# RMSNorm with GELU on one core: the first group's store in two pieces, gamma in four transfers, the last group in four stores

## The chip, the cores and the metric

One NeuronCore of one Trainium2 chip. The metric is the device time of the slowest core in microseconds (us), here of the only core. A lower number is better. The profile is of one execution; its "span" is from the first to the last instruction.

## The reference

x is 8 x 1024 x 2048 in float32, gamma has 2048 elements.

```python
rms = np.sqrt(np.mean(x ** 2, axis=-1, keepdims=True) + eps)
out = gamma * x / rms
return 0.5 * out * (1 + np.tanh(np.sqrt(2 / np.pi) * (out + 0.044715 * out ** 3)))
```

67.1 MB are read and 67.1 MB written; nothing of that can be saved.

## The kernel before

The 8192 rows are cut into 16 groups of 128 partitions x 4 rows. A partition's four rows are 32 KB in one piece, in memory and in the slot. There are six slots. SP issues the loads on one DMA queue, ACT gamma and the stores on another.

```python
store_pieces = {G - 1: [(0, 2), (2, 2)]}          # last group: two stores of 2 MiB

def load(g):
    nc.sync.dma_start(out=slot[g % SLOTS], in_=x3[g])
# ... squares (ACT), inverse_rms (POOL), scale by gamma (DVE)
def gelu_store(g):
    for r, n in store_pieces.get(g, [(0, R)]):
        for q in range(r, r + n):
            # ... Gelu of row q on ACT, in place
        nc.scalar.dma_start(
            out=o3[g, :, r : r + n, :], in_=slot[g % SLOTS][:, r : r + n, :]
        )

with tc.manual_schedule():
    for g in range(SLOTS):
        load(g)
    nc.scalar.dma_start(                            # gamma: one transfer of 8 KB
        out=gamma_row[:, :, 0:GW],
        in_=gamma.rearrange("(o a b) -> o a b", o=1, b=GW),
    )
    # ... memsets, gamma spread over the partitions by matmuls
    for g in range(G + 1):
        if g < G:
            squares(g); inverse_rms(g); scale(g)    # (one statement per line in the kernel)
        if g:
            gelu_store(g - 1)
            if g - 1 + SLOTS < G:
                load(g - 1 + SLOTS)
```

Of the kernel before, what the change touches and what calls it, by code (L numbers as in the profile page):

```python
# [1 line left out]

# [4 lines left out]

FP32 = mybir.dt.float32
ALU = mybir.AluOpType
ACT = mybir.ActivationFunctionType  # L10

P = 128
ROWS = 4
SLOTS = 6

GW = 128


@with_exitstack
def kernel(  # L20
    ctx: ExitStack,
    tc: tile.TileContext,
    x: bass.AP,
    gamma: bass.AP,
    eps: bass.AP,
    out: bass.AP,
):




    nc = tc.nc
    D = x.shape[-1]
    R = ROWS
    eps_f = float(eps)
    x3 = x.rearrange("b s d -> (b s) d").rearrange("(g p r) d -> g p r d", p=P, r=R)
    o3 = out.rearrange("b s d -> (b s) d").rearrange("(g p r) d -> g p r d", p=P, r=R)
    G = x3.shape[0]

    sbuf = ctx.enter_context(tc.tile_pool(name="sbuf", bufs=1))  # L40
    psum = ctx.enter_context(
        tc.tile_pool(name="psum", bufs=1, space=bass.MemoryType.PSUM)
    )
    slot = [sbuf.tile([P, R, D], FP32, name=f"slot{i}") for i in range(SLOTS)]
    gamma_row = sbuf.tile([1, D // GW, GW + 16], FP32, name="gamma_row")
    ones = sbuf.tile([1, P], FP32, name="ones")
    warm = sbuf.tile([1, 1], FP32, name="warm")
    power = sbuf.tile([P, R], FP32, name="power")
    ssq = sbuf.tile([P, G, R], FP32, name="ssq")
    rstd = sbuf.tile([P, G, R], FP32, name="rstd")  # L50
    ms = sbuf.tile([P, R], FP32, name="ms")
    y = sbuf.tile([P, R], FP32, name="y")
    z = sbuf.tile([P, R], FP32, name="z")
    gamma_ps = psum.tile([P, D], FP32, name="gamma_ps")
    junk = psum.tile([P, D], FP32, name="junk")

    store_pieces = {G - 1: [(0, 2), (2, 2)]}
    scale_pieces = {G - 1: [(0, 1), (1, 1), (2, 1), (3, 1)]}

    def load(g):  # L60
        nc.sync.dma_start(out=slot[g % SLOTS], in_=x3[g])  # L61

    def squares(g):
        for r in range(R):
            nc.scalar.activation(  # L65
                out=junk,
                in_=slot[g % SLOTS][:, r, :],
                func=ACT.Square,
                accum_out=ssq[:, g, r : r + 1],
            )  # L70

    def scale(g):
        for r, n in scale_pieces.get(g, [(0, R)]):
            rows = slot[g % SLOTS][:, r : r + n, :]
            nc.vector.tensor_tensor(  # L75
                out=rows,
                in0=rows,
                in1=gamma_ps.unsqueeze(1).to_broadcast([P, n, D]),
                op=ALU.mult,
            )  # L80

    def inverse_rms(g):

        v = nc.gpsimd
        v.tensor_scalar(  # L85
            out=ms, in0=ssq[:, g, :], scalar1=1.0 / D, scalar2=eps_f,
            op0=ALU.mult, op1=ALU.add,
        )
        v.tensor_tensor(out=y, in0=ms, in1=power, op=ALU.pow)  # L89
        v.tensor_tensor(out=z, in0=y, in1=y, op=ALU.mult)  # L90
        v.tensor_tensor(out=z, in0=z, in1=ms, op=ALU.mult)  # L91
        v.tensor_scalar(  # L92
            out=z, in0=z, scalar1=-0.5, scalar2=1.5, op0=ALU.mult, op1=ALU.add
        )
        v.tensor_tensor(out=rstd[:, g, :], in0=z, in1=y, op=ALU.mult)  # L95

    def gelu_store(g):
        for r, n in store_pieces.get(g, [(0, R)]):
            for q in range(r, r + n):
                row = slot[g % SLOTS][:, q, :]  # L100
                nc.scalar.activation(  # L101
                    out=row, in_=row, func=ACT.Gelu_apprx_tanh,
                    scale=rstd[:, g, q : q + 1],
                )
            nc.scalar.dma_start(  # L105
                out=o3[g, :, r : r + n, :], in_=slot[g % SLOTS][:, r : r + n, :]
            )

    with tc.manual_schedule():
        for g in range(SLOTS):  # L110
            load(g)
        nc.scalar.dma_start(
            out=gamma_row[:, :, 0:GW],
            in_=gamma.rearrange("(o a b) -> o a b", o=1, b=GW),
        )
        nc.gpsimd.memset(power, -0.5)  # L116
        nc.vector.memset(warm, 0.0)  # L117
        nc.vector.memset(ones, 1.0)  # L118
        nc.scalar.activation(out=warm, in_=warm, func=ACT.Gelu_apprx_tanh)  # L119
        for k in range(0, D, 512):  # L120
            nc.tensor.matmul(  # L121
                out=gamma_ps[:, k : k + 512],
                lhsT=ones,
                rhs=gamma_row[:, k // GW : (k + 512) // GW, 0:GW],
                start=True,
                stop=True,
            )
        for g in range(G + 1):
            if g < G:
                squares(g)  # L130
                inverse_rms(g)
                scale(g)
# [6 lines that stand above are left out]
# [1 line left out]
_INS = ['x', 'gamma', 'eps']  # L140
_OUTS = [((8, 1024, 2048), 'float32')]

_NUMBERS = {'eps': 9.999999747378752e-06}


# [26 lines left out]
```

## Time and profile before

| what | value |
|---|---|
| median, lowest, highest of the first three timed runs | 317.68, 317.36, 317.83 us |
| the profiled run | 318.66 us, span 316.9 us |
| ACT busy | 251.1 us (79%) |
| DMA, mean over the span | 424 GB/s |

The page's DMA row has one digit per fortieth of the span: 9 means that the 16 DMA engines were busy 90% or more. A line of the windows view has the stretch, its length, the busy time of PE, weight load, DVE, ACT and POOL with instruction counts, the granted clock, and last the DMA share and GB/s. A packet's whole time and all its bytes are counted in the window in which it starts, so a window much shorter than a packet's 1.2 us swings, and a share above 1 there does not mean that an engine does more than one packet at a time. The lines themselves are shown in the prediction.

### The profile page before, as it was taken

To read this page: it belongs to the slowest core of one execution; us is meant where nothing else is said; L and a number is where in the kernel's file an instruction comes from. 1 tells how busy PE (TensorE), PEld (TensorE's weight loads), DVE (VectorE), ACT (ScalarE), POOL (GpSimd) and SP (SyncE) were. 2 spreads that over 40 slices of the span, in tenths; PEclk is the share of its full clock that TensorE was granted. 3 is DMA by queue.
4 is the path that set the end of the run, shared out by engine and by line. 5 is a ranking of instruction groups with operands and counts; after the bars stand their busy time and mean duration, and the time that the engine had idled before them with its cause. 6 is when DMAs were issued, how large, how long until landed. Compare 5 with 4: busy or idle time off the path is not lost.

```text
span 316.9 us, 473 instructions
## 1 busy us (share of the span) xinstructions
PE 7.2 (2%) x8; PEld 2.5 (1%) x8; DVE 139.4 (44%) x21; ACT 251.1 (79%) x194; POOL 32.3 (10%) x101
## 2 busy tenths in 40 slices
PE   0900000000000000000000000000000000000000
PEld 0300000000000000000000000000000000000000
DVE  0038909090919191732808246091550905582000
ACT  1379999999999997959689595995959859599800
POOL 0020102020202020202002020020200102001000
DMA  8999999999999999999999999999999999999995
GB/s 328 414 451 426 434 393 459 401 459 402 459 405 455 426 434 431 430 434 426 438 426 455 410 455 418 443 426 430 434 430 435 422 459 405 459 414 447 422 420 230
DMA packets 4787, 134.25 MB, mean 424 GB/s; under 512 B 544, under 2 KB 560, under 8 KB 560
## 3 DMA queue, kind: packets, MB, share of 16 engines
q1 hardware_dynamic: 2304, 67.11, 49.5%
q10 hardware_dynamic: 2480, 67.12, 49.1%
q14 instruction: 3, 0.02, 0.0%
HBM read 67.12 MB, written 67.11 MB: 424 GB/s over the span
## 4 chain that ended last, share of the span: by engine, by line
DMA 56%; ACT 33%; issue 5%; ACTq 1%; SPq 0%
DMA slot<-in_x_dram 30%; DMA out_dram<-slot 26%; ACT slot L101 19%; ACT junk L65 14%; ACTq L105 1%; SPq L61 0%; ACTq L101 0%; ACTq L65 0%
## 5 line engine op out<-in xcount | busy, mean ns | idle before, releaser
L75 DVE TENSOR_TENSOR slot<-slot,gamma_ps 128x8192 f32<-128x8192 f32 (+1 forms) x19 | 139.2, 7340 | 147.0 <-ACT junk L65 147.0
L65 ACT ACTIVATE junk<-slot 128x2048 f32<-128x2048 f32 x64 | 120.4, 1881 | 47.3 <-DMA slot<-in_x_dram 43.7
L101 ACT ACTIVATE slot<-slot,rstd 128x2048 f32<-128x2048 f32 x64 | 122.8, 1989 | 0.9 <-ACT slot L101 0.9
L85 POOL TENSOR_SCALAR ms<-ssq 128x4 f32<-128x4 f32 x16 | 3.1, 194 | 247.5 <-ACT junk L65 247.5
L89 POOL TENSOR_TENSOR y<-ms,power 128x4 f32<-128x4 f32 x16 | 16.1, 1009 | 1.3
L65 ACT ACTIVATION_READ_ACCUMULATOR junk<-slot 128x1 f32 x64 | 12.0, 188 | 0.0
L121 PE MATMUL gamma_ps<-gamma_row,ones 1*128 1x512 f32 x8 | 7.2, 1072 | 8.4 <-DMA gamma_row<-in_gamma_dram 8.4
L95 POOL TENSOR_TENSOR rstd<-z,y 128x4 f32<-128x4 f32 x16 | 3.2, 201 | 1.3
L91 POOL TENSOR_TENSOR z<-z,ms 128x4 f32<-128x4 f32 x16 | 3.2, 201 | 1.3
L90 POOL TENSOR_TENSOR z<-y 128x4 f32<-128x4 f32 x16 | 3.2, 199 | 1.3
L92 POOL TENSOR_SCALAR z<-z 128x4 f32<-128x4 f32 x16 | 3.1, 194 | 1.4
L121 PEld LDWEIGHTS gamma_ps<-gamma_row,ones 1*128 1x128 f32 x8 | 2.5, 325 | 11.5 <-issue 11.5
L119 ACT ACT_TABLE_LOAD x1 | 1.3, 1283 | 1.3 <-PEq L153 1.3
L117 DVE MEMSET warm<- 1x1 f32 x1 | 0.1, 59 | 0.8 <-PEq L153 0.8
L119 ACT ACTIVATE warm<-warm 1x1 f32<-1x1 f32 x1 | 0.2, 202 | 0.0
L118 DVE MEMSET ones<- 1x128 f32 x1 | 0.2, 165 | 0.0
L116 POOL MEMSET power<- 128x4 f32 x1 | 0.1, 102 | 0.3 <-POOLq L153 0.3
L153 POOL MEMSET const-float32-0.0<- 128x1 f32 x1 | 0.1, 99 | 0.2 <-issue 0.2
L153 POOL MEMSET const-bfloat16-1.0<- 128x1 bf16 x1 | 0.1, 102 | 0.0
L153 POOL MEMSET const-uint8-127<- 128x1 uint8 x1 | 0.1, 102 | 0.0
L153 POOL MEMSET const-float32-1.0<- 128x1 f32 x1 | 0.1, 99 | 0.0
## 6 DMA issues: line engine op xcount, KB each, us to landing
slot<-in_x_dram SPq DMA_DIRECT2D x16, 4096.0 KB, 37.1
out_dram<-slot ACTq DMA_DIRECT2D x15, 4096.0 KB, 38.6
out_dram<-slot ACTq DMA_DIRECT2D x2, 2048.0 KB, 15.0
gamma_row<-in_gamma_dram ACTq DMA_DIRECT2D x1, 8.0 KB, 7.5
```

The source lines that it names most:

```text
L65: nc.scalar.activation(out=junk, in_=slot[g % SLOTS][:, r, :], func=ACT.Square, accum_out=ssq[:, g, r : r + 1],)
L75: nc.vector.tensor_tensor(out=rows, in0=rows, in1=gamma_ps.unsqueeze(1).to_broadcast([P, n, D]), op=ALU.mult,)
L85: v.tensor_scalar(out=ms, in0=ssq[:, g, :], scalar1=1.0 / D, scalar2=eps_f, op0=ALU.mult, op1=ALU.add,)
L89: v.tensor_tensor(out=y, in0=ms, in1=power, op=ALU.pow)
L90: v.tensor_tensor(out=z, in0=y, in1=y, op=ALU.mult)
L91: v.tensor_tensor(out=z, in0=z, in1=ms, op=ALU.mult)
L92: v.tensor_scalar(out=z, in0=z, scalar1=-0.5, scalar2=1.5, op0=ALU.mult, op1=ALU.add)
L95: v.tensor_tensor(out=rstd[:, g, :], in0=z, in1=y, op=ALU.mult)
L101: nc.scalar.activation(out=row, in_=row, func=ACT.Gelu_apprx_tanh, scale=rstd[:, g, q : q + 1],)
L105: nc.scalar.dma_start(out=o3[g, :, r : r + n, :], in_=slot[g % SLOTS][:, r : r + n, :])
L119: nc.scalar.activation(out=warm, in_=warm, func=ACT.Gelu_apprx_tanh)
L121: nc.tensor.matmul(out=gamma_ps[:, k : k + 512], lhsT=ones, rhs=gamma_row[:, k // GW : (k + 512) // GW, 0:GW], start=True, stop=True,)
```

## The change

The intent: let stores begin on small rows, get gamma in pieces so that the first matmul can start earlier, and let the last stores go out row by row.

```diff
-GW = 128
+GW = 32
+CHUNK = 512
+NARROW = 128
...
-    store_pieces = {G - 1: [(0, 2), (2, 2)]}
+    whole = [(R, [(0, R * D)])]
+    store_pieces = {
+        0: [(R, [(0, NARROW), (NARROW, R * D)])],
+        G - 1: [(1, [(r * D, r * D + D)]) for r in range(R)],
+    }
...
+            for a, b in stores:
+                nc.scalar.dma_start(out=dst[:, a:b], in_=flat[:, a:b])
...
     with tc.manual_schedule():
+        for k in range(0, D, CHUNK):
+            nc.scalar.dma_start(
+                out=gamma_row[:, k // GW : (k + CHUNK) // GW, 0:GW],
+                in_=gamma[k : k + CHUNK].rearrange("(o a b) -> o a b", o=1, b=GW),
+            )
         for g in range(SLOTS):
             load(g)
-        nc.scalar.dma_start(
-            out=gamma_row[:, :, 0:GW],
-            in_=gamma.rearrange("(o a b) -> o a b", o=1, b=GW),
-        )
```

More of the change, by code (lines that the diff above doesn't have):

```diff
@@ L44 @@
     slot = [sbuf.tile([P, R, D], FP32, name=f"slot{i}") for i in range(SLOTS)]
-    gamma_row = sbuf.tile([1, D // GW, GW + 16], FP32, name="gamma_row")
+    gamma_row = sbuf.tile([1, D // GW, GW + 4], FP32, name="gamma_row")
     ones = sbuf.tile([1, P], FP32, name="ones")
@@ L97, in gelu_store @@
     def gelu_store(g):
-        for r, n in store_pieces.get(g, [(0, R)]):
-            for q in range(r, r + n):
-                row = slot[g % SLOTS][:, q, :]
+        flat = slot[g % SLOTS].rearrange("p r d -> p (r d)")
+        dst = o3[g].rearrange("p r d -> p (r d)")
+        row = 0
+        for n, stores in store_pieces.get(g, whole):
+            for r in range(row, row + n):
                 nc.scalar.activation(
-                    out=row, in_=row, func=ACT.Gelu_apprx_tanh,
-                    scale=rstd[:, g, q : q + 1],
-                )
+                    out=slot[g % SLOTS][:, r, :],
+                    in_=slot[g % SLOTS][:, r, :],
+                    func=ACT.Gelu_apprx_tanh,
+                    scale=rstd[:, g, r : r + 1],
+                )
+            row += n
+            for a, b in stores:
+                nc.scalar.dma_start(out=dst[:, a:b], in_=flat[:, a:b])
+    with tc.manual_schedule():
+        for k in range(0, D, CHUNK):
             nc.scalar.dma_start(
-                out=o3[g, :, r : r + n, :], in_=slot[g % SLOTS][:, r : r + n, :]
+                out=gamma_row[:, k // GW : (k + CHUNK) // GW, 0:GW],
+                in_=gamma[k : k + CHUNK].rearrange("(o a b) -> o a b", o=1, b=GW),
             )
-    with tc.manual_schedule():
         for g in range(SLOTS):
             load(g)
-        nc.scalar.dma_start(
-            out=gamma_row[:, :, 0:GW],
-            in_=gamma.rearrange("(o a b) -> o a b", o=1, b=GW),
-        )
         nc.gpsimd.memset(power, -0.5)
@@ L119 @@
         nc.scalar.activation(out=warm, in_=warm, func=ACT.Gelu_apprx_tanh)
-        for k in range(0, D, 512):
+        for k in range(0, D, CHUNK):
             nc.tensor.matmul(
-                out=gamma_ps[:, k : k + 512],
+                out=gamma_ps[:, k : k + CHUNK],
                 lhsT=ones,
-                rhs=gamma_row[:, k // GW : (k + 512) // GW, 0:GW],
+                rhs=gamma_row[:, k // GW : (k + CHUNK) // GW, 0:GW],
                 start=True,
```

## The prediction

> **What bounds the kernel now.** I read the page first, then the waits, then windows of the trace, coarse in the middle and fine at the start and the end, then the packet records behind them, and last the compiled order of instructions of both kernels. From the page:
>
> ```profile
> span 316.9 us, 473 instructions
> PE 7.2 (2%) x8; PEld 2.5 (1%) x8; DVE 139.4 (44%) x21; ACT 251.1 (79%) x194; POOL 32.3 (10%) x101
> ...
> DMA  8999999999999999999999999999999999999995
> ...
> q1 hardware_dynamic: 2304, 67.11, 49.5%
> q10 hardware_dynamic: 2480, 67.12, 49.1%
> q14 instruction: 3, 0.02, 0.0%
> ```
>
> No compute engine is full, ACT has 66 us to spare, and the DMA row is full in every slice but the first and the last. Loads (q1) and stores (q10) halve the 16 engines. The waits say the same: ACT waits for loads, and the load queue for stores, which free the six slots.
>
> ```profile
> ACT junk L65 <- DMA slot<-in_x_dram: 43.7, 11, 10.3
> ```
> ```profile
> SPq L61 <- DMA out_dram<-slot: 222.0, 10, 50.7
> ```
>
> So the question is only whether 16 DMA engines are ever idle or slow. Windows (last two columns: DMA share, GB/s):
>
> ```profile
> 49.00:68.40 19.40, 0.00 (x0) 0.00 (x0) 11.99 (x2) 18.89 (x15) 2.46 (x9) 1.00 1.01 434
> 107.20:204.20 97.00, 0.00 (x0) 0.00 (x0) 43.44 (x5) 80.18 (x64) 9.98 (x30) 1.00 1.01 434
> 262.40:301.00 38.60, 0.00 (x0) 0.00 (x0) 17.57 (x5) 33.53 (x24) 4.00 (x12) 1.00 1.00 433
> ```
> ```profile
> 312.00:313.50 1.50, 0.00 (x0) 0.00 (x0) 0.00 (x0) 0.00 (x0) 0.00 (x0) 1.00 0.69 295
> 313.50:314.50 1.00, 0.00 (x0) 0.00 (x0) 0.00 (x0) 0.00 (x0) 0.00 (x0) 1.00 0.12 49
> 314.50:315.50 1.00, 0.00 (x0) 0.00 (x0) 0.00 (x0) 0.00 (x0) 0.00 (x0) 1.00 0.04 16
> 315.50:316.90 1.40, 0.00 (x0) 0.00 (x0) 0.00 (x0) 0.00 (x0) 0.00 (x0) 1.00 0.00 0
> ```
>
> In the middle it is 433 to 434 GB/s, no dent. At the end most engines stop by 313.5; share 0.12 is two engines of 16, 0.04 less than one. Two engines are late, and the last one sets the end. The packet records agree: fourteen engines move their last data by 313.5, one at 314.5, one at 315.5; the span ends 1.3 us later. Where the late one fell behind shows at the first store (issued at 38.6):
>
> ```profile
> 41.00:42.00 1.00, 0.00 (x0) 0.00 (x0) 0.00 (x0) 0.97 (x2) 0.00 (x0) 1.00 1.77 524
> 42.00:43.00 1.00, 0.00 (x0) 0.00 (x0) 0.00 (x0) 1.00 (x2) 0.00 (x0) 1.00 0.23 98
> 43.00:44.00 1.00, 0.00 (x0) 0.00 (x0) 0.00 (x0) 0.97 (x2) 0.00 (x0) 1.00 1.01 426
> ```
>
> A packet is one partition's 32 KB row and normally takes 1.213 us. At 41.2 to 43.3 fifteen engines spend about 1.75 us on one load packet, then alternate store and load. One engine spends 2.38 and 1.54 us on two load packets in a row, and starts its first store packet at 45.4, where the others start their second. It finishes store 0 at 63.5, the others by 61.7, and it is 2.0 us behind them at the end too.
>
> **The sum that makes 317.7.** Each engine moves 8 rows x 16 groups x 2 directions = 256 packets x 1.213 = 310.5 us. It starts at about 1.9, and its first packet takes some 0.75 longer than later ones: 313.2, which is where the fourteen end. Add 2.3 for the latest engine and 1.3 from its end to the span's end: 316.9. The median time, 317.68, is 0.8 above the span.
>
> **What the Trainium skill says.**
> 1. "DMA: Bandwidth & Descriptors", section "Where 436 GB/s comes from": 435.2 GB/s is the ceiling of the SBUF ports. The trace agrees, 432 to 434: a transfer can't be made faster here, only idle and uneven ends can be taken away.
> 2. Same page, "Queues, rings and completion order": an engine takes turns between queues packet by packet, some 9 to 17 descriptors in each. The turns are there from 43 us on; but gamma's 512 B packet at 6.1 us and its 4 B completion are parted by a whole 32 KB load packet, so here a turn is one row. I use the measured turn.
> 3. Same page, "Rules for kernel authors": at least 1 MiB for full rate, under 64 KB mostly overhead. The four last stores are 1 MiB, the narrow store 64 KB. The trace shows little fixed cost where the queue is backed up: 16 KB packets take 0.611, twice that is 1.222 against 1.213.
> 4. "Perfetto Trace Analysis", "DMA Optimizations": splitting lets work start sooner if DMA engines are generally idle. Here they are not, which speaks against a gain from the four stores.
>
> **The change, part by part.**
>
> *Gamma in four transfers, first in program order.* ACT issued gamma at 0.72 before too, since the loads are on another queue. It costs three more issues of 0.33 to 0.6 us, while ACT is idle until 13.1. Four data and four completion packets per engine, one per load turn of 1.24 us from 6.1 on: the last chunk lands near 6.1 + 7 x 1.24 + 0.5 = 15.3, and two matmul passes (2.1) end at 17.4. DVE first reads the result at 21.3. Hidden. DMA cost at most 3 x 27 ns.
> There are eight completion semaphores, and in the new order loads 4 and 5 each wait for a gamma chunk: issued by about 13 instead of 3.5, while loads 0 to 3 keep the queue busy until 41.8. Hidden.
>
> *Narrow store first.* Eight packets of 512 B per engine. One per turn, with the completion, gives 9 x (1.213 + 0.027) = 11.2 us in which loads have nearly the whole rate; the rest of store 0 starts near 43 + 11 = 54. So load 4 should land near 52 to 54 instead of 61.7, and store 0 complete near 71 to 73 instead of 63.5. Load 6 waits for that slot: issued near 72 to 74 instead of 63.6. Load 5 is done near 69, so the load queue runs dry for some 5 us; store 1 (issued near 55) fills the engines meanwhile. Bytes are only reordered, the loads stay about 6 us ahead, and nothing is idle. Own cost 8 x 27 ns = 0.22, less 8 x 19 ns for the shorter rows.
> What it can give: an engine that misses its first store turn now loses a 27 ns packet, not a 1.21 us one. I expect the 2 us laggard gone. The second laggard (1.0 us) grows by 0.4 to 0.5 just after 76 and 239, where the instruction queue has 8 KB packets of 0.31 us; that is not touched and then sets the end. Gain 315.5 - 314.5 = 1.0. The common stretch of 0.54 us (1.75 - 1.21) at the first store may also shrink, as gamma's small packets at 6 us stretched one neighbour by only 0.09; I count half, 0.25.
>
> *Four last stores.* Two more issues on ACT, each with its restart 0.42 us as in the timeline (300.6 is now the last issue): the last store is issued at 301.5. The engines need it only 8 x 0.31 = 2.5 us before 313.5, at 311. Before, they needed the last one at 308.6 and had it at 301. Slack on both sides: no gain, no wait. 8 KB packets: I take 0.309 from the instruction queue's, so 32 x 0.309 against 16 x 0.611 = +0.11 us.
>
> *Six more ACT-queue DMAs* (24 against 18), completion packets of 9 ns: +0.05.
>
> Sum of costs 0.08 + 0.07 + 0.11 + 0.05 = 0.3; of gains 1.25. 317.7 + 0.3 - 1.25 = 316.75; I say 316.8.
>
> **Rivals.**
> *All unevenness goes.* Both laggards at 313.5 and the stretch gone: 317.7 - 2.0 - 0.5 + 0.3 = 315.5. For it: the small packets may let every engine start its stores in step. Against: the instruction fetches stay.
> *Nothing is gained.* The stretch and the missed turn come when the first full-size store packet meets a load packet, at 54 instead of 43, or again when loads resume at 74. Then costs alone remain: 318.0. For it: the first load packets at 1.9 us show the same stretch with no second queue.
> *The delay upsets the loop.* Store 0 frees its slot some 10 us late. If loads then came late to ACT at the end, the last stores would be exposed. Against: load 15 has to land more than 5 us later than 276.2 to use up the slack before 308.6, and I expect it earlier. A dry spell with both queues empty might cost 1 to 3 us: 319 to 321.
> *The tail gets several us shorter from finer stores.* Against: it is not waiting for data, the stores are backed up from 275 on.
>
> **Range and chances.** The floor with everything even is about 315.1 (313.5 - 0.5 + 1.3 + 0.8), and 2% is 6.35 us: even it is 0.8% away, so faster by 2% is out of reach unless the packet rate itself rises. Slower by 2% needs 6.3 us of DMA idleness, which only a loop upset could give. So 0.98 within, 0.005 faster, 0.015 slower. Range 315.4 to 318.2: from the first rival to the second, a little wider above.
>
> **What would show it.** Right: steady windows still at 432 to 434; load 4 lands near 53; store 0's rest lands near 72 and load 6 is issued just after; last stores issued by 301 to 302 with the queue still full; in the end windows one late engine, not two, and the last data near 314.5. Wrong: a window with share well under 0.9 between 50 and 300 (loop upset); stores starting at once at 43 (rows of the narrow store taken in one turn); the late engine still 2 us behind (missed turn only moved); or a steady rate other than 433.

## The result, and the profile after

| | before | after |
|---|---|---|
| median of four runs | 317.52 us | 317.47 us |
| lowest to highest | 317.36 to 317.83 | 317.24 to 317.90 |
| span of the profiled run | 316.9 | 315.5 |

The ratio is 0.9999, with a 95% interval of 0.9982 to 1.0016: the same. A ratio is the mean time of one kernel's fast runs over that of the other's of the same rounds, so it is not quite the ratio of the medians.

The two spans differ by 1.4 us and the medians by 0.05. From the page of the kernel after:

```profile
span 315.5 us, 479 instructions
PE 7.9 (3%) x8; PEld 2.1 (1%) x8; DVE 139.4 (44%) x21; ACT 251.2 (80%) x194; POOL 32.3 (10%) x101
...
DMA  8999999999999999999999999999999999999997
...
q1 hardware_dynamic: 2304, 67.11, 49.7%
q10 hardware_dynamic: 3008, 67.12, 49.4%
```

The bound is the same: DMA full in all slices but the ends. The 528 packets more on q10 are the narrow rows, the smaller last rows, gamma and completions. The waits of ACT and of the load queue:

```profile
ACT junk L73 <- DMA slot<-in_x_dram: 36.8, 10, 8.7
```
```profile
SPq L69 <- DMA out_dram<-slot: 224.3, 10, 53.7
...
SPq L69 <- DMA gamma_row<-in_gamma_dram: 10.2, 2, 7.9
```

The last line is new. Completion semaphores are used in rotation, and loads 4 and 5 had to wait until a gamma piece landed. It cost nothing, as loads 0 to 3 kept the queue busy until 42. Steady windows and the end:

```profile
107.20:204.20 97.00, 0.00 (x0) 0.00 (x0) 45.34 (x6) 84.17 (x68) 11.60 (x34) 1.00 1.00 432
262.40:301.00 38.60, 0.00 (x0) 0.00 (x0) 15.55 (x5) 29.11 (x19) 2.36 (x8) 1.00 1.00 432
```
```profile
312.00:313.50 1.50, 0.00 (x0) 0.00 (x0) 0.00 (x0) 0.00 (x0) 0.00 (x0) 1.00 0.88 371
313.50:314.50 1.00, 0.00 (x0) 0.00 (x0) 0.00 (x0) 0.00 (x0) 0.00 (x0) 1.00 0.08 33
314.50:315.50 1.00, 0.00 (x0) 0.00 (x0) 0.00 (x0) 0.00 (x0) 0.00 (x0) 1.00 0.00 0
```

No engine is still moving data after 314.5. Before, 312.0 to 313.5 had 295 GB/s and there was some until 315.5. So the data finish more evenly, not earlier: the packet records give the mean over the 16 engines of their last completion, 313.49 before and 313.56 after, while the latest is 315.55 and 314.30. The first store now looks like this. First its two issues on ACT (`ACTq`), then windows:

```profile
31.07 3.88 ACT L111 ACTIVATE slot<-slot,rstd 128x2048 f32<-128x2048 f32 x2
33.09 0.36 ACTq L119 DMA_DIRECT2D out_dram<-slot  x1
34.85 3.88 ACT L111 ACTIVATE slot<-slot,rstd 128x2048 f32<-128x2048 f32 x2
38.77 0.34 ACTq L119 DMA_DIRECT2D out_dram<-slot  x1
```
```profile
36.40:46.00 9.60, 0.00 (x0) 0.00 (x0) 3.48 (x1) 9.09 (x9) 0.00 (x0) 1.00 1.05 444
46.00:47.00 1.00, 0.00 (x0) 0.00 (x0) 0.00 (x0) 1.00 (x1) 0.00 (x0) 1.00 1.54 489
47.00:48.00 1.00, 0.00 (x0) 0.00 (x0) 0.71 (x1) 1.00 (x3) 0.58 (x2) 1.00 0.21 66
48.00:49.00 1.00, 0.00 (x0) 0.00 (x0) 1.00 (x1) 1.00 (x1) 0.84 (x3) 1.00 1.20 486
```

From 36.4 to 46 the narrow rows and the loads share the engines without loss. Then the rest of group 0 arrives in full rows, and the dip that stood at 42 to 43 before (98 GB/s) stands at 47 to 48 (66 GB/s). It has moved, not gone. A dip is not idleness: by the packet records the engines stay at work through it (all 16 before, at least 14 at any instant after), on load packets that take longer than usual, so that few new ones start.

Three numbers of each run carry the rest of this document. *Stretch* is by how much packets took longer than the usual packet of their size (1.213 us for 32 KB, 1.194 for the 31.5 KB rows, 0.611 for 16 KB, 0.309 for 8 KB, and the usual time of each other size), summed and divided by 16. *Mean end* and *latest end* are of the engines' last completions. All are tallied from the packet records of each trace.

| run | stretch, first loads | stretch, first stores | mean end | latest end | span |
|---|---|---|---|---|---|
| before, first profile | 0.72 | 0.63 | 313.49 | 315.55 | 316.9 |
| after, first profile | 0.71 | 0.67 | 313.56 | 314.30 | 315.5 |
| e1 before again | 0.77 | 0.80 | 313.59 | 314.31 | 315.7 |
| e2 gamma only | 0.62 | 0.78 | 313.46 | 314.32 | 315.7 |
| e3 narrow only | 0.68 | 0.59 | 313.29 | 314.02 | 315.4 |
| e4 four stores only | 0.65 | 0.69 | 313.63 | 314.77 | 316.2 |
| f1 after again | 0.68 | 0.84 | 313.70 | 314.64 | 315.8 |
| f2 one last store | 0.75 | 0.68 | 313.55 | 314.26 | 315.5 |
| f3 first piece 8 KB | 0.64 | 0.60 | 313.29 | 313.90 | 315.3 |
| f4 graded | 0.67 | 0.61 + 0.72 | 314.14 | 315.09 | 316.4 |
| g1 narrow again | 0.61 | 0.57 | 313.30 | 314.00 | 315.4 |
| g2 first piece 8 KB, timed | 0.77 | 0.62 | 313.30 | 314.08 | 315.5 |
| g3 narrow first load | 0.68 | 0.82 | 314.06 | 315.81 | 317.2 |
| g4 one queue | 0.73 | 0.64 + 1.5 | 315.79 | 317.62 | 318.9 |

### The profile page after: what moved, and what is told of

It is laid out like the page before. It is cut to its first block, busy times and chain, and to the rows that moved or that the text cites. A ratio compares the mean times of both kernels' runs of the same rounds, so it can differ in the third digit from the quotient of the medians.

```text
span 315.5 us, 479 instructions
## 1 busy us (share of the span) xinstructions
PE 7.9 (3%) x8; PEld 2.1 (1%) x8; DVE 139.4 (44%) x21; ACT 251.2 (80%) x194; POOL 32.3 (10%) x101
## 4 chain that ended last, share of the span: by engine, by line
ACT 38%; DMA 32%; another core or an unknown queue 18%; issue 5%; ACTq 1%; SPq 0%
ACT slot L111 21%; DMA slot<-in_x_dram 16%; ACT junk L73 16%; DMA out_dram<-slot 15%; ACTq L119 1%; SPq L69 0%; ACTq L111 0%; ACTq L73 0%
## 5 line engine op out<-in xcount | busy, mean ns | idle before, releaser
L134 PE MATMUL gamma_ps<-gamma_row,ones 1*128 1x512 f32 x8 | 7.9, 1112 | 9.2 <-DMA gamma_row<-in_gamma_dram 9.2
```

The lines of the kernel that those rows point to most:

```text
L134: nc.tensor.matmul(out=gamma_ps[:, k : k + CHUNK], lhsT=ones, rhs=gamma_row[:, k // GW : (k + CHUNK) // GW, 0:GW], start=True, stop=True,)
```

## The experiments

Twelve kernels, in three calls, each on another chip, with runs of the kernel before among them. My theory after the result (A): both kernels give the 16 engines the same work, and the late engine of the first profile was a chance event of that one execution, not part of the median. The rival (B): the late engine belongs to the kernel before, and the change cures it in each run. After the first call a third joined (C): it comes in some runs only, and small first rows make it rarer.

The kernels e2 to f4, g1 and g2 were written as the changed kernel with its other parts put back. The cuts below are abridged and show only the part that counts, against the kernel before unless they say otherwise. All timed runs are in the fast state; f3 and f4 have a single run each, whose state is unknown.

### e1: the kernel before, against itself

No edit.

> The kernel before, unchanged, against itself. Theory A (chance): the engine that ended 2.0 us after the rest in the first profile of before belongs to that one execution (it took 318.66 us where other runs of the same kernel took 317.36 to 317.83). Then most spans of these runs lie at 315.5 to 316.3 and at most one in five is near 316.9; the ratio to before is 1.000 within 0.002. Theory B (systematic): the late engine is part of this kernel, and the change cures it. Then nearly every span here is 316.5 to 317.2, about 1 us above the 315.5 to 316.1 of the changed kernel.

Measured: 317.43 median of six, 317.25 to 318.79; ratio 0.9992 (0.9967 to 1.0017). Five spans lie between 315.5 and 316.1 and one is 317.0. The eleven runs of the kernel before beside it fall into two heaps: six from 317.12 to 317.43 and five from 318.05 to 319.07. Here is the end of this profile:

```profile
312.00:313.50 1.50, 0.00 (x0) 0.00 (x0) 0.00 (x0) 0.00 (x0) 0.00 (x0) 1.00 0.79 339
313.50:314.50 1.00, 0.00 (x0) 0.00 (x0) 0.00 (x0) 0.00 (x0) 0.00 (x0) 1.00 0.04 16
314.50:315.50 1.00, 0.00 (x0) 0.00 (x0) 0.00 (x0) 0.00 (x0) 0.00 (x0) 1.00 0.00 0
```

It is the same kernel as in the prediction, without the late engine. In every run of both kernels the reported time is the span plus 1.7 to 1.8 us, so the 0.8 that I had taken from the median and the first profile's span was a difference between two executions. Theory B is refuted. A is right about the median. Its "at most one in five" holds for these six runs (one), but with the eleven beside them it is six of 17, so long runs are more frequent than that. Clock and state are the same in both heaps.

### e2, e3, e4: each part alone

```diff
 # e2: only gamma (GW = 32; this line stands for the loop shown under "The change")
+        for k in range(0, D, CHUNK): nc.scalar.dma_start(gamma piece k), before the loads
 # e3: only the narrow first store
+        0: [(R, [(0, NARROW), (NARROW, R * D)])],
 # e4: only the last group in four
+        G - 1: [(1, [(r * D, r * D + D)]) for r in range(R)],
```

> Only gamma in four transfers, first in program order; stores as before. Theory A: nothing is exposed, the time is that of before within 0.3 us (ratio 0.999 to 1.001), the first large DVE product starts at 21 to 22 us as before, although the last gamma piece lands near 14 to 15. Theory B: no cure of the late engine here, span like before.

> Only the narrow first store; gamma and last stores as before. Theory A: same time within 0.4 us; narrow packets run from about 36 to 46 us without stretching the loads, the stretch of about 0.65 us per engine comes when the first full row of the rest is taken, near 46 to 48, as large as before. Theory B: the cure of the late engine sits here, spans 1 us under those of before.

> Only the last group in four stores. Theory A: cost 0.1 us of packets, no gain, since the stores before it are backed up: ratio 0.999 to 1.002; the last store is issued near 301.5 and its data are written from about 311 on. A rival (tail): if the end waited for the last store, this alone would save 1 to 2 us.

Measured:

| | median of six | lowest to highest | over 318 us | ratio to before |
|---|---|---|---|---|
| e2 gamma | 317.37 | 317.21 to 317.69 | 0 | 0.9983 (0.9961 to 1.0005) |
| e3 narrow | 317.48 | 317.20 to 317.87 | 0 | 0.9986 (0.9964 to 1.0009) |
| e4 four stores | 317.93 | 317.42 to 318.33 | 2 | 1.0000 (0.9974 to 1.0025) |

Each is within noise. In e2 the first large DVE product starts at 21.67, against 21.27 before. In e3 the engines end at 313.29 in the mean, 0.2 to 0.3 earlier than in the two profiles of before. e4's last store is issued at 301.84, as the prediction had it, and nothing comes earlier. Four of its six runs are below 318 us and still mostly above the usual 317.4 (317.42, 317.67, 317.90, 317.95), so its higher median does not come of long runs alone; with six runs it is within noise. The rival that the tail waits for the last store is refuted here and again in f2.

### f1: the changed kernel again

No edit.

> The changed kernel again, beside more runs of the kernel before. So far 7 of 22 runs of the kernel before took over 318 us, and 0 of 11 of the two kernels with the narrow first store. Theory A (chance alone): the changed kernel too has about a third of its runs over 318 us; medians alike within 0.3 us. Theory C (the narrow store makes the late engine rarer): 0 or 1 of 6 runs over 318, while the kernel before has again 3 or more of 11; the medians still alike, the mean lower by 0.2 to 0.4 us.

Measured: 317.57 median of five, 317.32 to 317.65, none over 318; before 317.41, 317.23 to 318.19, one of nine over 318; ratio 0.9999 (0.9986 to 1.0013). C's forecast for the changed kernel holds, its forecast of three or more among the runs of before does not. (A slip: the count "0 of 11" took the profiled run twice; it was 0 of 10. In the same way "none of 17" in g1 should read 16.)

### f2: the last group in one store

```diff
-        G - 1: [(2, [(0, 2 * D)]), (2, [(2 * D, 4 * D)])],
+        G - 1: [(R, [(0, R * D)])],          # 4 MiB in one store
```

> The kernel before with the last group as one store of 4 MiB instead of two of 2 MiB: it is issued near 301, and the engines are done with the store before it near 303.5. If the stores are backed up as I read it, there is no bubble or one of under 1 us, and the time is within 0.6 us of before. If the end waits for the last issue, it costs 4 us or more against before (a 4 MiB store takes 9.7 us from about 303 on, if the engines were idle before).

Measured: 317.29 median of four (317.14 to 318.95), ratio 1.0006 (0.9982 to 1.0029). The store is issued at 299.81, just in time, and the engines never pause:

```profile
303.00:312.00 9.00, 0.00 (x0) 0.00 (x0) 0.00 (x0) 0.00 (x0) 0.00 (x0) 1.00 1.00 430
```

One, two or four last stores give the same time within noise, because the stores before them are backed up: in f2's packet records all 16 engines are at work at every instant from 300 to 312.

### f3 and g2: a first piece of 8 KB

Against e3, the narrow store alone:

```diff
-NARROW = 128
+NARROW = 2048
```

> As the narrow store alone, but the first piece has 8 KB per partition instead of 512 B. The piece is issued after the first row, near 33, and starts near 36.5. If the stretch of about 0.65 us per engine belongs to the first store rows of any real size, it moves to 36 to 40, and none is left at 46 to 50. If it belongs to full 32 KB rows against loads, it stays where the rest starts. If it grows with the size, there are two smaller ones. The sum over both is what counts: 0.6 to 0.8 expected, so no gain.

> First piece of 8 KB per partition, timed: the single look had 317.08. If that was a gain, the median is 317.0 to 317.2 and below that of before in every round; if it was the low end of the same spread, the median is 317.3 to 317.5, ratio to before 0.998 to 1.001. The count of long runs goes with that of the narrow store.

Measured: f3 317.08 in its single look, g2 317.26 median of six (317.16 to 317.56), ratio 0.9980 (0.9959 to 1.0002). The stretch is neither moved nor left in place: it is spread in small pieces from 35 to 52 us, and sums to 0.60 and 0.62. Bringing the store in more gently does not make it cheaper. The 317.08 was the low end of the spread.

### f4: five stores of growing size

Against e3:

```diff
-        0: [(R, [(0, NARROW), (NARROW, R * D)])],
+        0: [(R, [(0, 128), (128, 640), (640, 2176), (2176, 4224), (4224, R * D)])],
```

> First group in five stores, of 512 B, 2 KB, 6 KB, 8 KB and 15.5 KB per partition. Each takes 8 turns and a completion, so group 0 is stored much later, load 6 issued past 75, and the load queue runs dry. If what counts is only that one queue always has work, the span stays 315.5 to 316.5. If a dry load queue costs (loop upset), the span is over 317.5. The stretch at the first stores: under 0.4 us per engine if a gradual start avoids it, 0.6 or more if not.

Measured: 318.15 in one look, span 316.4, mean end 314.14; between the two forecasts. The first stretch is 0.61, as large as always, but it does not fall on the first stores: the rows of 512 B and 2 KB cost nothing (0.00 from 36 to 54), and it falls on load packets that start from 59 to 62, among the 6 KB rows. Loads 0 to 5 are all in by 63.7, load 6 is issued at 72.1 and moves its first rows at 75.9. In between stores alone use the engines and lose nothing, and the return of the loads shows next to none either (0.03 from 72 to 80). But from 84.3 to 88, where the engines pass from store 1 to store 2, their load packets mostly take 1.5 to 2.1 us, a second stretch of 0.72:

```profile
64.00:84.00 20.00, 0.00 (x0) 0.00 (x0) 12.27 (x2) 19.16 (x15) 3.30 (x11) 1.00 1.03 440
84.00:85.00 1.00, 0.00 (x0) 0.00 (x0) 1.00 (x1) 1.00 (x1) 0.00 (x0) 1.00 1.34 524
85.00:86.00 1.00, 0.00 (x0) 0.00 (x0) 1.00 (x1) 1.00 (x2) 0.00 (x0) 1.00 1.24 360
86.00:87.00 1.00, 0.00 (x0) 0.00 (x0) 1.00 (x1) 1.00 (x1) 0.00 (x0) 1.00 0.56 164
```

Then the rate is 433 again. The mean end is 0.55 to 0.65 later than in the two profiles of before, which is about this stretch. So in this run a dry load queue is not a loss in itself while stores have work. That the second stretch comes of the disturbed order is likely, since no other two-queue run has it, but what makes it at that hand-over is open.

### g1: the narrow store alone, again

> Narrow store alone, again, for the count of long runs (over 318 us). So far: 11 of 47 runs of kernels whose first store has full rows, none of 17 of kernels whose first store has 512 B or 8 KB rows. If the narrow store makes the late engine rarer, 0 or 1 of 6 here. If chance, 1 or 2 of 6. Median 317.2 to 317.6 either way; mean end of the 16 engines 313.2 to 313.7.

Measured: 317.30 median of six, 317.18 to 317.47, none over 318. Of the eleven runs of before in the same call, five took 318.20 to 319.19. Ratio 0.9981 (0.9957 to 1.0004). C is borne out. The trace has a lone engine: its first full store row comes at 48.82, the others' by 47.21, after load packets stretched by 1.26, and it loses nothing more; this run took 317.18.

### g3: a narrow first load

```diff
-        nc.sync.dma_start(out=slot[g % SLOTS], in_=x3[g])
+        for a, b in [(0, 128), (128, R * D)] if g == 0 else [(0, R * D)]:
+            nc.sync.dma_start(out=flat[:, a:b], in_=src[:, a:b])
```

> The kernel before with the first load split into 512 B per partition and the rest. The first packets of the loads are stretched by 0.62 to 0.77 us per engine in every run so far. If a short first row takes the stretch away, the mean end of the engines is 312.9 or earlier and the span 0.6 us shorter. If the stretch is a fixed time until data flow, it stays, in the narrow packets or the first full ones, and the time does not change (ratio 0.998 to 1.001).

Measured: 319.35 median of four (318.72 to 320.55), ratio 1.0049 (1.0018 to 1.0079); 0.5% longer, clear of noise, which neither guess had. The short rows run between 1.7 and 2.3 us of the trace; the first full rows start in the mean at 2.48 instead of 1.92, and then show the usual stretch, 0.68. So the mean end is 0.5 later. More comes from one engine that ends at 315.81, and 0.25 lies outside the span (the time is the span plus 2.0 to 2.1 here). That engine does what the late engine of the prediction did: it takes two load packets before its first store row, stretched by 1.29 us, and loses another 1.78 later, nearly all on load packets. A second engine does the first of these too (1.10) and ends at 314.92. Why all four runs are long here I did not find out.

### g4: stores on the load queue

```diff
-            nc.scalar.dma_start(
+            nc.sync.dma_start(            # stores; gamma stays on ACT
...
-                if g - 1 + SLOTS < G:
-                    load(g - 1 + SLOTS)
+                if g >= 3 and g - 3 + SLOTS < G:
+                    load(g - 3 + SLOTS)
```

> Stores issued on the load queue, each load two groups later than its slot's store so that the queue always holds work; gamma alone stays on the other queue. If the stretch of 0.6 to 0.8 us per engine comes from a second queue joining a busy one, it is gone near 41 us and there is none when stores follow loads near 61; the mean end of the engines is 312.8 to 313.0, and the span 0.5 us shorter if nothing runs dry. If it comes from the first store rows as such, it appears near 61. If one queue in order holds up something else, the windows between 60 and 290 show a DMA share under 0.95 and the time grows by several us.

Measured: 320.67 median of four (320.37 to 320.89), ratio 1.0085 (1.0058 to 1.0112).

```profile
41.00:51.00 10.00, 0.00 (x0) 0.00 (x0) 4.38 (x1) 9.94 (x9) 1.99 (x6) 1.00 0.99 429
54.00:61.00 7.00, 0.00 (x0) 0.00 (x0) 1.30 (x1) 6.91 (x8) 0.00 (x0) 1.00 0.96 374
61.00:290.00 229.00, 0.00 (x0) 0.00 (x0) 112.97 (x16) 190.52 (x148) 25.85 (x78) 1.00 1.00 431
290.00:300.00 10.00, 0.00 (x0) 0.00 (x0) 0.16 (x1) 10.00 (x6) 0.00 (x0) 1.00 0.92 396
```

There is no stretch at 41, but 0.64 near 55 to 61, on the last load rows before the first stores, which follow in the same queue. So it is not a second queue that costs, but the coming of the first stores. And since the queue now turns from loads to stores and back all the time, there are later stretches of 0.05 to 0.34, 1.5 us in all after 90, which the two queues in alternation don't have. From 290 to 300 the engines also wait for the last stores to be issued: from 288 to 302 each stands idle for 0.9 us in the mean. This and the 1.5 about make up the 2.3 by which the mean end is later.

### The count of long runs

| first store | runs | over 318 us | median | mean |
|---|---|---|---|---|
| kernel before | 42 | 13 | 317.44 | 317.80 |
| e2, e4, f2 (full first rows too) | 16 | 3 | | |
| changed kernel | 9 | 0 | 317.51 | 317.51 |
| narrow or 8 KB first rows (e3, g1, f3, g2) | 19 | 0 | 317.32 | 317.36 |

16 of 58 against 0 of 28: were the rates equal, so lopsided a split would come about once in 1,200 (16 of 86 drawn at random, all from the 58). The limit of 318 was chosen after the first call; the two later calls alone have 7 of 24 against 0 of 18, about 1 in 80. Drawn within each call, as calls differ, it is about 1 in 1,600 for all and 1 in 160 for the two later calls. All this takes the runs of a call as independent, which was not tested. f4 (318.15) and g3 (all four over 318) are left out, as each lost time in a way of its own. The three calls ran on three chips, and the share of long runs of the kernel before was 1 of 9 in one call, 5 of 11 in another and, with e1, 6 of 17 in the first.

So small first store rows very likely make the long runs rarer. Two limits: most of the weight is in the runs of the narrow store alone, for the changed kernel itself ran in calls where before had few long runs (0 of 9 against 3 of 18 of kernels with full first rows beside it). And e2, with gamma in four pieces and full first rows, had 0 of 6 long runs too, in a call where before had 6 of 17; whether that is luck was not tested.

How it works is not shown: of the kernels counted here only one long run was traced, that of the prediction. In it one engine, alone, takes two load packets before its first store, stretched by 1.49 us, and loses another 1.47 in many small pieces later, nearly all on load packets from 82 on; the other fifteen lose 0.01 to 0.49 there. In the traced runs of the changed kernel eleven and seven engines take their first full store row later than the others, and none loses as much there (0.85 and 1.28 at most). f2's trace has a lone engine too (first store row at 44.60, the others by 43.77; stretched by 0.98, another 1.01 lost later, on store packets), and its time was 317.33; g1's lost 1.26 and nothing later. A lone engine is thus not enough.

## Why the prediction was right or wrong

The predicted time was 316.8, the range 315.4 to 318.2, with 0.98 for "within 2%". The measured 317.47 lies in it. But the sum had a net gain of 0.95 in it (1.25 less 0.3) that the median doesn't show: the measured gain is 0.05, and the interval (0.6 faster to 0.5 slower) excludes it. The number is in the range only because the range reached to the rival in which nothing is gained. One of the signs I had named came true by luck: the last data of the profile after are at 314.30, near my 314.5, but they are at 314.31 in e1, the unchanged kernel. Step by step:

- **The bound** was right. 432 to 434 GB/s in every steady window of both kernels, no compute engine busier than ACT's 80%. I quoted the skill's 435.2 GB/s as the ceiling and left out that the same section, "Where 436 GB/s comes from", has the HBM side, about 358 GB/s, bind for transfers between HBM and SBUF. The measured 432 to 434 lies above that, with the program on one core.
- **"The sum that makes 317.7"** failed in its last line. It joined a span of 316.9 from a run of 318.66 to a median of 317.68. In every run of both kernels the difference is 1.7 to 1.8 us, so the median run of before has a span near 315.7 and no late engine.
- **"Gain 315.5 - 314.5 = 1.0"** is therefore the mis-sized term. The narrow store alone does seem to make such runs rarer, as I argued, but 13 of 42 runs of before were long, not all, so the median gains nothing. The mean can: 317.50 against 317.81 in e3's call (e1 counted with before) and 317.30 against 318.02 in g1's. For the changed kernel itself no gain of the mean is shown: 317.49 against 317.52 in f1's call, the only one after the prediction in which it ran; the pooled 317.51 against 317.80 compares different calls.
- **The second late engine** was read rightly. In the trace after, the engine that ends last (314.30) is the one that carried two of the three instruction packets, 0.62 us, and it has 0.45 us of later stretch, beside them. The same holds in e2, e3, f1 and g1.
- **"The common stretch ... I count half, 0.25"** was wrong, it is 0. 0.67 after against 0.63 before, and 0.57 to 0.84 in all variants with two queues. The rival "the stretch and the missed turn come when the first full-size store packet meets a load packet" had the stretch right for this change, at 46 and not at 54 (f4 shows that 6 KB rows bring it too). Its +0.3 us lies in the measured interval, my -0.9 does not.
- **The costs of 0.3** were right. The usual packet times of all packets sum to 310.93 per engine before and 311.19 after, so 0.26.
- **"The rest of store 0 starts near 54"** was wrong. I read the order of ACT's instructions as the time of issue. The narrow piece needs only the first row's GELU and was issued at 33.1, while ACT was still on the later rows; its eight turns ran from 36.5 to 45, mostly before full rows could have started. The rest began at 46.8 to 49.0, load 4 landed at 58.3 and not near 53, store 0 at 67. The load queue did not run dry: load 6 was issued at 67.4, load 5 landed at 77.6. The loads end 4.5 us earlier than before (271.2 against 275.8), not 6.
- **Gamma and the four last stores** were right: both hidden. The last matmul ends near 17.1, DVE first needs it at 21.6. The last store of the changed kernel is even issued at 297.05, because of the earlier loads, and is still not waited for.
- **"The delay upsets the loop"** did not occur, but f4, which disturbs the loop far more, lost some 0.7 us (318.15 in its one run, median of before 317.41), where I had said 1 to 3, and not for a dry queue.

The section "DMA Optimizations" of the Trainium skill's page "Perfetto Trace Analysis" has it that splitting may help if DMA engines are generally idle. One, two and four last stores (medians 317.29, 317.44, 317.93; each within noise of before in its own call) agree: here they are not idle, and it doesn't.

What stays open: why one engine sometimes goes on losing time for 200 us after a late start, why g3 makes this regular, and what the engines do in the stretch itself, of which f4 shows a second that I can't place.

The lowest mean of the kernels is that of the small first piece alone, without the other two parts: 317.36 over 19 runs (512 B or 8 KB), against 317.80 of the kernel before and 317.51 of the changed one, over different calls. In its own calls the ratios are 0.9980 to 0.9986 with intervals that just reach over 1, and e2's six runs do as well (mean 317.39, ratio 0.9983). This is a more even kernel rather than a faster one.

## What to carry to other kernels

Before you build on a feature of a profile, ask whether the profiled run was a typical one: compare its own reported time with the timed runs, and look at how many of them share it. Where all DMA engines are busy, as here, look first at the mean end of the engines: no finer cut at the start or the end moved it earlier by more than 0.3 us, and the latest end differed by 1.2 us between two runs of one kernel. Small rows on the first transfer of a second direction can still be worth trying, for fewer long runs. And compare means only within a call: the share of long runs differed from call to call.

## What the Trainium skill lacked or had wrong

- "DMA: Bandwidth & Descriptors", section "Queues, rings and completion order": a packet of some 9 to 17 descriptors per turn. Here a turn is one row, be it 32 KB or 512 B. In the changed kernel each engine's eight 512 B rows are parted by a load packet each, so 64 KB took from 36.5 to 45.
- No page that I read has the loss when the other direction first joins: 0.57 to 0.84 us per engine when stores first join loads, in two queues or in one (g4), and 0.60 to 0.62 in sum where the first rows have 8 KB. It falls on load packets, mostly those just before the first full store rows; rows of 512 B and 2 KB joined without it (f4, 0.00).
- No page that I read has a size for how unevenly engines with equal bytes end on these queues ("DMA: Bandwidth & Descriptors" says only that engines finish independently, and calls two of them usually slower, with DMAs issued from GpSimd as its guess at the cause): 312.9 to 315.55 in one run of the kernel before, 313.2 to 314.3 in another. Part of it are the instruction packets of 8 KB, 0.31 us each, two of three on one engine.
- Same page, "Rules for kernel authors", has under 64 KB as mostly overhead. The narrow store is at the edge of that, with 64 KB; with queues backed up it cost each engine 8 x 27 ns = 0.2 us, and nothing that the time shows.
- No page that I read has the constant part between span and reported time, 1.7 to 1.8 us here (2.0 in g3).
